# A hybrid HGRN2/retention step on one core: the first pass of each of the seven half-size products keeps its place in program order on TensorE

## The chip, the core and the metric

The kernel runs on one core of one Trainium2 chip. The metric is the device time in microseconds (us), median of the runs; for the kernel before it is 1810.23 us over three runs (1810.15 to 1811.55).

## What is computed

Two layers of a backbone over 640 tokens (128 context tokens and 512 latent tokens, five tiles of 128), each with a token mixer and a SwiGLU feed-forward part. The mixer is cut here; the change lies in the feed-forward part of the second layer:

```python
def layer(x, cond, s0_h, s0_r, pos, p):
    ...
    y, S_a, S_b = token_mixers(h, p, s0_h, s0_r, pos)
    x = x + g_m * y
    h = rmsnorm(x, p["norm_ffn"]) * (1.0 + sc_f) + sh_f
    gate, up = jnp.split(h @ p["w_up"], 2, axis=-1)
    x = x + g_f * ((jax.nn.silu(gate) * up) @ p["w_down"])
    return x, S_a, S_b
```

`w_up` has 1024 rows and 2 x 2816 columns, that is 22 blocks of 128 columns for `gate` and 22 for `up`; everything is float32.

## The kernel before, in words

Every float32 operand of a large product is held as a pair of a rounded part and a rest (`wh` and `wl` for weights, the planes 0 and 1 of `hT`, or the pairs `eh`, for activations). A product of two such pairs is three matmuls: rounded by rounded, rounded by rest, rest by rounded. Weights come by DMA into `raw`, ScalarE (ACT) casts them into `wh` (L104), and VectorE (DVE) subtracts to get `wl` (L105). Four buffers of each are kept (`W_BUFS`).

In the second layer `PLAIN` leaves two of the 22 column blocks to ordinary products. The other 20 go through `seven` (L701): the block of `gate` and the block of `up` for 640 tokens are one 2 x 2 arrangement of half-size blocks (half of the 1024 rows, half of the 640 tokens), computed with seven half-size products instead of eight. The price is sums and differences: of the tokens once per layer, of the weights by VectorE (`sums`, L113, four per block), and of the products by VectorE on their way out. `CH[1]` cuts the 22 blocks into groups of 6, 6, 5 and 5; the two ordinary blocks stand in the first group, so the groups hold 4, 6, 5 and 5 calls of `seven`. After each group `cols_512` (L1187) multiplies the group's activations by rows of `w_down`, in matmuls over 512 columns (L1200 to L1202), and `x_add` adds them to `x`.

One call of `seven` works in two PSUM tiles, `sx` and `sy`, each of 1024 columns. Products go to the columns 0 to 319 or 512 to 831 of one of them. Here they are called, in the order in which the code issues them:

- x0: first half of `sx`; ScalarE then copies it (L721).
- x1: second half of `sx`; VectorE then subtracts (L723, v2).
- y0: first half of `sy`; VectorE then subtracts (L726, v3).
- y1: second half of `sy`; VectorE then subtracts (L728, c22).
- x0': added onto the first half of `sx`; ScalarE then takes its SiLU (L731).
- x1': second half of `sx`, afresh; VectorE then subtracts (L733), ScalarE takes the SiLU (L734).
- y1': added onto the second half of `sy`; VectorE then subtracts (L738), multiplies (L741), and the result is split into a pair by L742 (ScalarE) and L743 (VectorE).

Each product is one call of `prod` (L710): four slices of 128 rows, with three matmuls (here: passes) of 320 columns each, at L713, L714 and L715; twelve passes a product, 84 a call, 1680 in all. `sx` and `sy` come from a pool of four such tiles, so two calls are in flight.

The order of the instructions on each engine is not that of the code: a scheduler of the build chooses it from what depends on what. A dependence between a pass and a reader of `sx` or `sy` becomes a wait of TensorE. `pin` (L351) names one instruction to the scheduler that is to keep its place in program order; before the change it is used on some instructions of VectorE and ScalarE (the weight sums at L113 among them) and on none of TensorE.

Of the kernel before, what the change touches and what calls it, by code (L numbers as in the profile page):

```python
# [148 lines left out]
class Net:  # L149
# [551 lines left out]
    def seven(self, act):  # L701
        nc, W, E = self.nc, self.W, self.E
        mm, V = nc.tensor.matmul, nc.vector
        X, Y, T = self.ps("sx"), self.ps("sy"), self.ON("sv")
        x0, x1, y0, y1 = X[:, :HALF], X[:, 512:512 + HALF], Y[:, :HALF], Y[:, 512:512 + HALF]
        v2, v3, c12, c22 = (T[:, i * HALF:(i + 1) * HALF] for i in range(4))
        sg = self.B("sgf")
        s1, s2 = sg[:, :HALF], sg[:, HALF:TOK]

        def prod(o, w, j, h, first=True):  # L710
            hi, lo = (x[:, HK * j:HK * j + HK] for x in w)
            for k in range(HK):
                mm(o, hi[:, k], h[0][:, k], start=first and k == 0, stop=False, skip_group_check=True)  # L713
                mm(o, hi[:, k], h[1][:, k], start=False, stop=False, skip_group_check=True)  # L714
                mm(o, lo[:, k], h[0][:, k], start=False, stop=k == HK - 1, skip_group_check=True)  # L715
            if j:
                W.done()
            return 5.1e-3 * HALF
        a = W.get(W.used)
        yield prod(x0, a, 0, self.quarter(0, 0))  # L720
        nc.scalar.copy(v2, x0)  # L721
        yield prod(x1, a, 1, E[2])
        V.tensor_tensor(v2, x1, v2, op=ALU.subtract)  # L723
        b = W.get(W.used)
        yield prod(y0, b, 0, E[3])
        V.tensor_tensor(v3, v2, y0, op=ALU.subtract)  # L726
        yield prod(y1, b, 1, E[1])
        V.tensor_tensor(c22, v3, y1, op=ALU.subtract)  # L728
        c = W.get(W.used)
        yield prod(x0, c, 0, self.quarter(0, 1), False)  # L730
        nc.scalar.activation(s1, x0, AF.Silu)  # L731
        yield prod(x1, c, 1, self.quarter(1, 1))
        V.tensor_tensor(s2, x1, v3, op=ALU.subtract)  # L733
        nc.scalar.activation(s2, s2, AF.Silu)  # L734
        d = W.get(W.used)
        cost = prod(y1, d, 0, E[4], False)
        W.done()
        V.tensor_tensor(c12, v2, y1, op=ALU.subtract)  # L738
        at = self.B("act", F32R).rearrange("p (d t) -> p d t", d=2)
        fv = sg[:, TOK:]  # L740
        V.tensor_tensor(fv, sg[:, :TOK], T[:, TOK:], op=ALU.mult)  # L741
        nc.scalar.copy(at[:, 0], fv)  # L742
        V.tensor_tensor(at[:, 1], fv, at[:, 0].bitcast(F32), op=ALU.subtract)  # L743
        act.append(at)
        yield cost
# [703 lines left out]
```

## Time and profile before

| what | value |
|---|---|
| median of 3 runs | 1810.23 us (1810.15 to 1811.55) |
| profiled execution, its own time | 1810.44 us |
| its span in the profile | 1808.7 us |
| TensorE (PE) busy | 1765.9 us, 98% of the span |
| VectorE (DVE) busy | 1192.8 us, 66% |
| ScalarE (ACT) busy | 763.7 us, 42% |
| mean granted clock of TensorE | 0.997 of full speed |

The profile gives busy time by engine, the chain of work that ended last, groups of instructions with what ended the idle time before them, and a timeline. The time of the execution is its span and 1.7 us around it. A matmul's row shows 0.31 us for a pass of 320 columns, but passes overlap; what one costs is the distance from its start to the start of the next.

### The profile page before, as it was taken

Reading aid. Unit: us, or ns where it says so; the run is one execution under the profiler, and the core shown is the slowest. Engines: PE = TensorE matmul, PEld = TensorE weight load, DVE = VectorE, ACT = ScalarE, POOL = GpSimd, SP = SyncE. Lnnn points to the kernel's source line nnn. Section 1 sums busy time; section 2 is a strip of 40 time slices with the busy share of each in tenths; the row PEclk is TensorE's granted clock in tenths of the full one; section 3 lists DMA queues with packets and bytes.
Section 4 is the critical chain, followed back from the end, with each engine's and each line's share of the span. In section 5 each row is a group of like instructions: output and inputs, shape, how many; then the busy total and the mean of one; then the engine's idle time right before and its main releaser. Section 6 shows DMA issues by size and latency. Waiting matters only on the chain.

```text
span 1808.7 us, 29243 instructions
## 1 busy us (share of the span) xinstructions
PE 1765.9 (98%) x12019; PEld 1678.3 (93%) x12019; DVE 1192.8 (66%) x1874; ACT 763.7 (42%) x1299; POOL 49.8 (3%) x59
## 2 busy tenths in 40 slices
PE   7999999999999999999999999999999999999997
PEld 5999899998999989999899999999999989899896
DVE  6787958864854666565676656475377667666766
ACT  7685445543422212222256555455354324233242
POOL 1100000000000000000000000000000000000000
PEclk9999999999999999999999999999999999999999
DMA  9414233221533444444442121211211312223131
GB/s 335 153 51 156 76 105 111 86 70 56 163 112 117 152 155 141 144 147 134 134 129 73 51 71 54 67 53 56 70 36 47 112 47 88 82 71 100 53 105 59
DMA packets 201622, 181.96 MB, mean 101 GB/s; under 512 B 7072, under 2 KB 171136, under 8 KB 201488
## 3 DMA queue, kind: packets, MB, share of 16 engines
q1 hardware_dynamic: 196592, 177.57, 31.3%
q10 hardware_dynamic: 4640, 2.43, 0.5%
q8 instruction: 94, 1.54, 0.3%
q0 software_dynamic: 256, 0.09, 0.1%
q14 instruction: 40, 0.33, 0.1%
HBM read 175.35 MB, written 4.72 MB: 100 GB/s over the span
## 4 chain that ended last, share of the span: by engine, by line
PE 75%; DVE 11%; ACT 5%; issue 4%; DMA 3%; POOL 1%; SPq 0%; DVEq 0%; POOLq 0%; ACTq 0%
PE gw L780 24%; PE ga L1200 6%; PE ga L1201 6%; PE ga L1202 6%; PE ga L826 4%; PE ga L825 4%; PE ga L824 4%; PE pl L917 3%; PE sx L713 2%; DVE wl L105 2%; PE sx L715 2%; PE sx L714 2%; ACT wh L104 2%; PE sy L713 1%; PE sy L714 1%
## 5 line engine op out<-in xcount | busy, mean ns | idle before, releaser
L104 ACT CAST wh<-raw 128x1024 fp32r<-128x1024 f32 (+1 forms) x265 | 265.2, 1001 | 644.9 <-PE gw L780 177.1
L105 DVE TENSOR_TENSOR wl<-raw,wh 128x1024 fp32r<-128x1024 f32 (+1 forms) x265 | 306.2, 1163 | 260.4 <-ACT wh L104 257.7
L780 PE MATMUL gw<-hT,wh 128*128 128x320 f32 x2432 | 461.8, 311 | 0.0
L780 PEld LDWEIGHTS gw<-hT,wh 128*128 128x128 f32 x2432 | 380.3, 188 | 0.6
L780 PE MATMUL gw<-hT,wl 128*128 128x320 f32 x1216 | 277.3, 309 | 0.0
L780 PEld LDWEIGHTS gw<-hT,wl 128*128 128x128 f32 x1216 | 203.1, 188 | 0.0
L824 PE MATMUL ga<-wh,hT 128*128 128x256 f32 x640 | 185.5, 290 | 0.0
L825 PE MATMUL ga<-wl,hT 128*128 128x256 f32 x640 | 181.3, 283 | 0.0
L826 PE MATMUL ga<-wh,hT 128*128 128x256 f32 x640 | 181.2, 283 | 0.0
L552 DVE CUSTOM_DVE_ANT_0 junk<-adt,srow 128x1024 f32<-128x1024 f32 x128 | 156.2, 1221 | 3.2 <-DMA adt<-in_ada_t 1.3
L1200 PE MATMUL ga<-wh,act 128*128 128x512 f32 x360 | 141.8, 394 | 0.0
L1201 PE MATMUL ga<-wl,act 128*128 128x512 f32 x360 | 140.5, 390 | 0.0
L1202 PE MATMUL ga<-wh,act 128*128 128x512 f32 x360 | 138.8, 390 | 0.0
L824 PEld LDWEIGHTS ga<-wh,hT 128*128 128x128 f32 x640 | 122.4, 191 | 0.1
L825 PEld LDWEIGHTS ga<-wl,hT 128*128 128x128 f32 x640 | 122.4, 191 | 0.1
L826 PEld LDWEIGHTS ga<-wh,hT 128*128 128x128 f32 x640 | 122.3, 191 | 0.0
L1200 PEld LDWEIGHTS ga<-wh,act 128*128 128x128 f32 x360 | 67.5, 188 | 17.4 <-DVE xa L1143 4.0
L713 PE MATMUL sx<-hT,wh 128*128 128x320 f32 x240 | 77.0, 322 | 4.0 <-DVE sv L723 4.0
L1202 PEld LDWEIGHTS ga<-wh,act 128*128 128x128 f32 x360 | 67.6, 188 | 14.1
L1201 PEld LDWEIGHTS ga<-wl,act 128*128 128x128 f32 x360 | 67.6, 188 | 13.4 <-DVE wl L105 0.6
L917 PE MATMUL pl<-X 128*128 128x128 f32 x560 | 72.9, 277 | 5.2 <-ACT X L904 5.1
L1143 DVE TENSOR_TENSOR xa<-ga,gate 128x512 f32<-128x512 f32 (+1 forms) x100 | 56.2, 580 | 32.9 <-PE ga L1202 17.0
(278 smaller groups left out, 3480.8 us busy)
## 6 DMA issues: line engine op xcount, KB each, us to landing
raw<-in_w_in SPq DMA_DIRECT2D x72, 512.0 KB, 3.8
adt<-in_ada_t SPq DMA_DIRECT2D x64, 512.0 KB, 3.8
raw<-in_w_up SPq DMA_DIRECT2D x48, 512.0 KB, 3.8
raw<-in_w_up SPq DMA_DIRECT2D x80, 256.0 KB, 3.0
raw<-in_w_down SPq DMA_DIRECT2D x39, 512.0 KB, 3.7
adw<-in_ada_w SPq DMA_DIRECT2D x16, 512.0 KB, 10.5
adw<-in_ada_w SPq DMA_DIRECT2D x32, 256.0 KB, 3.0
raw<-in_w_out SPq DMA_DIRECT2D x16, 512.0 KB, 3.7
```

What stands on the lines that cost most here:

```text
L104: nc.scalar.copy(hi[:, :n], raw[:, :n])
L105: nc.vector.tensor_tensor(lo[:, :n], raw[:, :n], hi[:, :n].bitcast(F32), op=ALU.subtract)
L552: r = V.tensor_tensor_reduce(out=self.junk, in0=w[:, :DM], in1=self.srow[c], scale=1.0, scalar=0.0, op0=ALU.mult, op1=ALU.add, accum_out=( ...
L713: mm(o, hi[:, k], h[0][:, k], start=first and k == 0, stop=False, skip_group_check=True)
L780: mm(o, w[:, k], self.hT[:, d, k, sl], start=k == 0 and i == 0, stop=k == KT - 1 and i == 2)
L824: mm(o, a_hi, hi[:, j], start=i == 0, stop=False)
L825: mm(o, a_hi, lo[:, j], start=False, stop=False)
L826: mm(o, a_lo, hi[:, j], start=False, stop=i == nk - 1)
L917: nc.tensor.matmul(pl[:, i * P:(i + 1) * P], X[:, TOK + i * P:TOK + (i + 1) * P], X[:, i * P:(i + 1) * P], start=True, stop=True)
L1200: mm(o, a_hi, hi[:, j], start=i == 0, stop=False)
L1201: mm(o, a_hi, lo[:, j], start=False, stop=False)
L1202: mm(o, a_lo, hi[:, j], start=False, stop=i == nk - 1)
```

## The change

The first pass of each product, the one at slice 0 of rounded by rounded, is given to `pin`. No instruction is added or removed.

```diff
@@ -710,7 +710,9 @@
         def prod(o, w, j, h, first=True):
             hi, lo = (x[:, HK * j:HK * j + HK] for x in w)
             for k in range(HK):
-                mm(o, hi[:, k], h[0][:, k], start=first and k == 0, stop=False, skip_group_check=True)
+                r = mm(o, hi[:, k], h[0][:, k], start=first and k == 0, stop=False, skip_group_check=True)
+                if k == 0:
+                    self.pin(r)
                 mm(o, hi[:, k], h[1][:, k], start=False, stop=False, skip_group_check=True)
                 mm(o, lo[:, k], h[0][:, k], start=False, stop=k == HK - 1, skip_group_check=True)
             if j:
```

L714 and L715 of the kernel before are L716 and L717 of the changed one, and all later lines are two higher.

How the order moves on TensorE is shown at three places of one call of `seven`, the fourth of the second group. Its tiles are `sx_14259` and `sy_14260`; `wh_14162` and `wl_14163` are the weights of x0 and x1, `14196`/`14197` those of y0 and y1, `14229`/`14230` those of x0' and x1', `14249`/`14250` those of y1'. What stands in brackets is the engine whose count the instruction waits for.

TensorE before, from the end of x0 to the beginning of x1:

```order
L715 MATMUL sx_14259<-hT_12371,wl_14163 128x320
L713 MATMUL sy_14260<-hT_12371,wh_14196 128x320
L714 MATMUL sy_14260<-hT_12371,wh_14196 128x320
L715 MATMUL sy_14260<-hT_12371,wl_14197 128x320 [waits DVE_49]
L713 MATMUL sy_14260<-hT_12371,wh_14196 128x320
L713 MATMUL sx_14259<-eh_12948,wh_14162 128x320 [waits Activation_49]
L714 MATMUL sx_14259<-eh_12949,wh_14162 128x320
```

TensorE in the changed kernel, the same place:

```order
L716 MATMUL sx_14259<-hT_12371,wh_14162 128x320
L717 MATMUL sx_14259<-hT_12371,wl_14163 128x320
L713 MATMUL sx_14259<-eh_12948,wh_14162 128x320 [waits Activation_49]
L716 MATMUL sx_14259<-eh_12949,wh_14162 128x320
L717 MATMUL sx_14259<-eh_12948,wl_14163 128x320
```

Four passes of y0 stood between the last pass of x0 and the first of x1, which waits for ScalarE; now none does.

TensorE before, from the end of y0 into x0':

```order
L714 MATMUL sy_14260<-hT_12371,wh_14196 128x320
L715 MATMUL sy_14260<-hT_12371,wl_14197 128x320
L713 MATMUL sx_14259<-hT_12371,wh_14229 128x320 [waits DVE_49]
L714 MATMUL sx_14259<-hT_12371,wh_14229 128x320
L715 MATMUL sx_14259<-hT_12371,wl_14230 128x320
```

Here y1 came only after eight passes of x0'. TensorE in the changed kernel, from the end of y0:

```order
L716 MATMUL sy_14260<-hT_12371,wh_14196 128x320
L717 MATMUL sy_14260<-hT_12371,wl_14197 128x320
L713 MATMUL sy_14260<-eh_12964,wh_14196 128x320 [waits DVE_49]
L716 MATMUL sy_14260<-eh_12965,wh_14196 128x320
L717 MATMUL sy_14260<-eh_12964,wl_14197 128x320
```

Now y1 follows y0 at once, with a wait for VectorE, and x0' comes after y1 with no wait.

TensorE before, from the end of x0' to the beginning of x1':

```order
L715 MATMUL sx_14259<-hT_12371,wl_14230 128x320
L713 MATMUL sx_14388<-hT_12371,wh_14290 128x320 [waits Activation_49]
L714 MATMUL sx_14388<-hT_12371,wh_14290 128x320
L715 MATMUL sx_14388<-hT_12371,wl_14291 128x320 [waits DVE_49]
L713 MATMUL sy_14260<-eh_12993,wh_14249 128x320 [waits DVE_49]
L714 MATMUL sy_14260<-eh_12994,wh_14249 128x320
L715 MATMUL sy_14260<-eh_12993,wl_14250 128x320
L713 MATMUL sx_14259<-hT_12371,wh_14229 128x320 [waits Activation_49]
```

TensorE in the changed kernel, the same place:

```order
L716 MATMUL sx_14259<-hT_12371,wh_14229 128x320
L717 MATMUL sx_14259<-hT_12371,wl_14230 128x320
L713 MATMUL sx_14259<-hT_12371,wh_14229 128x320 [waits Activation_49]
L716 MATMUL sx_14259<-hT_12371,wh_14229 128x320
L717 MATMUL sx_14259<-hT_12371,wl_14230 128x320
```

Three passes of the next call's x0 and three of y1' stood between x0' and x1'; now x1' follows x0' at once. In the changed program each of the 140 products stands as twelve passes in a row, in the order x0, x1, y0, y1, x0', x1', y1', but for the first call of the groups two to four, whose x0 is parted once by six passes of `cols_512`. In the last call of each group passes of `cols_512` still stand between products: five ahead of y1 in the first two groups and three in the last two, and three ahead of x1' in all four. On VectorE, in most calls, L738 now stands ahead of the subtraction of the 512-wide weights (L105) instead of behind it, and one L105 and one L113 changed places; on ScalarE one cast of the 20 at L742 moved by one place; the DMA queue of SyncE and GpSimd keep their order.

## Rows read from the trace of the kernel before

**Rows 1.** The page: engines' busy times; the weight subtraction L105 (busy, mean ns, idle before).

```profile
PE 1765.9 (98%) x12019; PEld 1678.3 (93%) x12019; DVE 1192.8 (66%) x1874; ACT 763.7 (42%) x1299; POOL 49.8 (3%) x59
...
L105 DVE TENSOR_TENSOR wl<-raw,wh 128x1024 fp32r<-128x1024 f32 (+1 forms) x265 | 306.2, 1163 | 260.4 <-ACT wh L104 257.7
```

**Rows 2.** One period: stretch, length, busy by engine (count), clock, DMA share, GB/s.

```profile
1508.26:1521.64 13.38, 12.95 (x84) 12.32 (x85) 10.37 (x16) 5.54 (x8) 0.00 (x0) 1.00 0.27 80
```

**Rows 3.** Tile sx, 1380 to 1770 us: what TensorE's idle time ended with (us, times).

```profile
  DVE sv L723: 11.1, 23
  ACT sv L721: 3.9, 20
  ACT sgf L731: 2.8, 16
```

**Rows 4.** Timeline, TensorE: end of x0, then first, second and twelfth x1 passes.

```profile
1517.19 0.31 PE L715 MATMUL sx<-hT,wl 128*128 128x320 f32 x1
...
1518.02 0.42 PE L713 MATMUL sx<-eh,wh 128*128 128x320 f32 x1
1518.27 0.31 PE L714 MATMUL sx<-eh,wh 128*128 128x320 f32 x1
...
1519.73 0.31 PE L715 MATMUL sx<-eh,wl 128*128 128x320 f32 x1
```

**Rows 5.** Timeline, ScalarE: the copy of x0 and the SiLU of x0'.

```profile
1517.54 0.43 ACT L721 COPY sv<-sx 128x320 f32<-128x320 f32 x1 [0.80 <-PE sx L715]
...
1525.73 0.43 ACT L731 ACTIVATE sgf<-sx 128x320 f32<-128x320 f32 x1
```

**Rows 6.** Timeline, TensorE and VectorE: end of y0, L723, two x0' passes.

```profile
1520.90 0.31 PE L715 MATMUL sy<-hT,wl 128*128 128x320 f32 x1
...
1521.10 0.48 DVE L723 TENSOR_TENSOR sv<-sx,sv 128x320 f32<-128x320 f32 x1
...
1521.64 0.41 PE L713 MATMUL sx<-hT,wh 128*128 128x320 f32 x1 [0.43 <-DVE sv L723]
1521.89 0.30 PE L714 MATMUL sx<-hT,wh 128*128 128x320 f32 x1
```

**Rows 7.** Timeline, TensorE: end of x0', first and second passes of x1'.

```profile
1525.11 0.31 PE L715 MATMUL sx<-hT,wl 128*128 128x320 f32 x1
...
1526.21 0.41 PE L713 MATMUL sx<-hT,wh 128*128 128x320 f32 x1
1526.46 0.31 PE L714 MATMUL sx<-hT,wh 128*128 128x320 f32 x1
```

**Rows 8.** Timeline: end of x1' (TensorE), its reader L733, and L726 (VectorE).

```profile
1527.92 0.31 PE L715 MATMUL sx<-hT,wl 128*128 128x320 f32 x1
...
1528.34 0.49 DVE L733 TENSOR_TENSOR sgf<-sx,sv 128x320 f32<-128x320 f32 x1 [1.26 <-PE sx L715]
...
1522.10 0.48 DVE L726 TENSOR_TENSOR sv<-sv,sy 128x320 f32<-128x320 f32 x1
```

**Rows 9.** Timeline, ScalarE: L721 of each group's first and last call.

```profile
1384.76 0.43 ACT L721 COPY sv<-sx 128x320 f32<-128x320 f32 x1
1423.96 0.43 ACT L721 COPY sv<-sx 128x320 f32<-128x320 f32 x1 [0.80 <-PE sx L715]
1478.03 0.43 ACT L721 COPY sv<-sx 128x320 f32<-128x320 f32 x1
1544.28 0.43 ACT L721 COPY sv<-sx 128x320 f32<-128x320 f32 x1 [0.80 <-PE sx L715]
1598.36 0.43 ACT L721 COPY sv<-sx 128x320 f32<-128x320 f32 x1 [0.36 <-PE sx L715]
1651.03 0.43 ACT L721 COPY sv<-sx 128x320 f32<-128x320 f32 x1 [0.80 <-PE sx L715]
1698.46 0.43 ACT L721 COPY sv<-sx 128x320 f32<-128x320 f32 x1 [0.36 <-PE sx L715]
1751.14 0.43 ACT L721 COPY sv<-sx 128x320 f32<-128x320 f32 x1 [0.80 <-PE sx L715]
```

## The prediction, written before the changed kernel ran

> **What bounds the kernel now.** I read the page first. TensorE is busy for 98% of the span [rows 1]. Work on other engines therefore matters only where TensorE stands still for it, and a change that adds or removes no instruction can only change those stands. The next view is one period of the stage that the change touches, from the first x0' pass of one call of `seven` to that of the next. It lasts 13.38 us for 84 passes, with VectorE busy for 10.37 us, ScalarE for 5.54 us, and the granted clock at 1.00, its 2.4 GHz level [rows 2]. So TensorE bounds this stage too, with 3 us of room on VectorE. Third, the idle time of TensorE around the tile `sx` names what it waits for: VectorE's L723 for 11.1 us, ScalarE's L721 for 3.9 us in all 20 calls, and L731 for 2.8 us in 16 [rows 3]. These sums understate a stand, since the pass after a wait is late as well. Therefore I price stands from the distances of the starts in the timeline.
>
> **A pass and its plain cost.** From the second to the twelfth pass of x1 ten starts take 1.46 us, 0.146 us each [rows 4].
>
> **The stands of a call before.** I take one call, the fourth of the second group.
> - x1 waits for L721, ScalarE's copy of x0. From the last x0 pass to the first x1 pass there are 0.83 us [rows 4]. Four y0 passes lie between, so five steps of 0.146 (0.73) are work and 0.10 is a stand. The next pass comes 0.25 us later instead of 0.146, another 0.10 [rows 4]. Together 0.20 us.
> - x0' waits for L723, the reader of x1. Between the last y0 pass and the first x0' pass there are 0.74 us, a stand of 0.59 us, and 0.25 us to the second pass, 0.10 more [rows 6]. Together 0.70 us. L723 was late: it began 1.37 us after the last x1 pass [rows 4, 6].
> - x1' waits for L731, the reader of x0'. With six passes between there are 1.10 us, seven steps are 1.02, so 0.08 and again 0.10 for the second pass [rows 7]. Together 0.18 us.
> - y1 and y1' cost nothing: eight passes of x0' and longer pieces cover their readers.
>
> Sum 1.08 us. The period without stands is 13.38 - 1.08 = 12.30 us, which is 84 passes of 0.146.
>
> **What the change removes.** The stand of x0' goes entirely: x0' now follows y1, and y1's wait for L726 already implies that L723 is done, since both are VectorE's and L723 comes first. That is 0.70 us less per call. The piecemeal stands at x1 and x1' (0.20 and 0.18) go in their present form.
>
> **What the change adds.** The waits are the same as before; what moves is what stands ahead of the waiting pass. TensorE works in order, so everything behind that pass waits with it, the other tile's products and the next call's included.
> - x1 directly behind x0. The path is: ScalarE begins L721 0.35 us after the last x0 pass has begun, needs 0.43 us, and x1 begins 0.05 us later, 0.83 us in all [rows 4, 5]. None of the four passes lies in it any more, so the stand is 0.83 - 0.146 = 0.68, plus 0.10 for the second pass: 0.79 us.
> - x1' directly behind x0'. L731 takes 0.43 us, and x1' begins 0.05 us after its end [rows 5, 7]. Its reader is on ScalarE as well and would begin 0.35 us after the last pass, as L721 did: again 0.79 us. The cast that kept ScalarE busy ahead of L731 waits for weights that y1 frees; with all twelve x0' passes now behind y1, it is over before x0' is.
> - y1 directly behind y0. The trace never shows VectorE free at this place, so I price it by the nearest rows. VectorE's L733 begins 0.42 us after the last pass of its product; L726 takes 0.48 us [rows 8]; the waiting pass begins 0.06 us after VectorE's end, as x0' did after L723 [rows 6]. That is 0.96 us, a stand of 0.81, and with 0.10 for the second pass 0.92 us. The lower bound is ScalarE's response of 0.35 in place of 0.42. The upper bound lets L723 be as late as now, 1.37 us after x1's last pass: then L726, which came 1.00 us behind L723 with one weight sum between them [rows 6, 8], begins at 2.37, where y0 (twelve passes, 1.75 us, and 0.42) would allow 2.17. So up to 0.2 us more. I take 0.92, because the stands themselves give VectorE more time ahead of L723.
> - y1' behind x1': its reader L728 has all of x0' and x1' (24 passes, 3.5 us) and the stand at x1' to finish. Nothing. The swaps of L105 and L113 with L728 and L738 on VectorE fall in the same cover; if it were gone, the price would be one L105, 1.16 us on average [rows 1], a call.
> - x0 of the next call and y0 use tiles and weights freed a call or more ago. Nothing.
>
> New stands: 0.79 + 0.92 + 0.79 = 2.50 us. The new period is 12.30 + 2.50 = **14.80 us**, 1.42 over the steady one of before.
>
> **The sum.** Not all calls were steady. From the first to the last L721 of the four groups there are 39.20, 66.25, 52.67 and 52.68 us, 210.80 us for 16 periods, 13.18 on average [rows 9]. Now 16 x 14.80 = 236.8 us: **+26.0**. The first x1 of each group lies outside these periods: 4 x (0.79 - 0.20) = **+2.4**. In the last call of each group wide passes still stand ahead of y1 and x1'. Passes of 512 columns, by columns, would take 0.146 x 512/320 = 0.23 us (an estimate from the row), so three cover 0.7 and five 1.2 us; what is left is 0 to 0.2 us each, about what these places cost before: **0**. Uncovered they would be 4 x 1.7 = 6.8 us, the upper bound.
>
> Together +28.4 us. The profiled execution took 1810.44 us, so 1838.8; the median of the runs lies 0.2 us below it, so **1838.6 us**. No later stage can give this back: the wide products that follow run on TensorE too.
>
> **Rivals.**
> - *The waits don't bind (faster).* Place: the first pass of x1, x1' and y1. The two products of a tile lie in different halves of it, so the reader of one half need not hold up writes to the other. If the waits were met by the time TensorE arrives, only the gain would be left: the decisive point is a reader's path below 0.146 us instead of 0.83. Then a period is 12.30: 16 x 12.30 = 196.8, 14.0 below 210.8, and 4 x 0.20 less at the first calls: 1810.23 - 14.8 = 1795.4 us. For it speaks that the halves are disjoint. Against it: with four passes in between, x1 stood in all 20 calls [rows 3], and began just behind the reader's end [rows 4, 5]. Chance 0.04. The Trainium skill, PSUM — Partial Sum Buffer, section "PSUM bank collisions raise a hardware error", asks for a guard "by bank × quadrant", and by its bank of 512 fp32 values the two halves lie in different banks. By that rule alone these waits would not be needed, and the time would be this rival's; the row shows that the program waits all the same, by tile.
> - *VectorE falls behind (much slower).* If the new order lets one more weight subtraction (1.16 us, [rows 1]) stand ahead of L726 or L728 when TensorE needs it, each call pays 0.2 to 1.16 us more: 1842.6 to 1861.8 us. For it speaks L723's lateness now; against it VectorE's 10.37 us in a period that grows to 14.80. Chance 0.10, of which I leave 0.06 beyond my range.
> - *Nothing changes.* If the moved stands only replaced each other, or the order on the chip's queue made no difference, the time would be 1810 us. The rows of the order speak against it: the passes that covered the waits are gone at all 20 calls. Chance 0.03.
>
> **How the numbers follow.** The forecast has 0.83, the rivals 0.04, 0.10 and 0.03. If the late second pass came only half as often as assumed, 20 x 3 x 0.05 = 3 us fall away; if never, 6 us; with the faster response at y1 20 x 0.07 = 1.4 us: low end 1831. Upward, 0.2 us at y1 in 20 calls are 4 us, and most of the uncovered last calls 5 us: high end 1848. Outside lie the faster rival, no change and the worse part of the second, 0.13 together, and some error of pricing. A measurement of this kernel can tell about 0.2%, 3.6 us, from no change. Faster 0.04, the same 0.03, slower 0.93.
>
> **What would show it.** In the changed profile the period of `seven` should be near 14.8 us; the idle ahead of L713 should name L721, L731 and now L726 some 20 times each, with about 0.5 us or more a time, and L723 no longer; the number of passes and the pitch of 0.146 should stay; the granted clock should stay at 1.00. A step is wrong if x1 begins less than 0.8 us behind x0's last pass, if L726 begins more than 0.5 us behind y0's last pass, or if y1' waits. The prediction is wrong if the period stays at or under 13.4 us.

## The result, and the profile after

The changed kernel takes 1836.81 us (median of 4 runs, 1836.49 to 1837.19) against 1810.19 us of the kernel before (4 runs): a ratio of 1.0146, 95% interval 1.0128 to 1.0163, or 26.6 us more. The forecast was 1838.6 us. The profiled execution spans 1835.1 us, 26.4 more than before.

The head of the page of the changed kernel, with span, busy times, share of the span and number of instructions:

```profile
span 1835.1 us, 29217 instructions
...
PE 1767.4 (96%) x12019; PEld 1675.6 (91%) x12019; DVE 1192.2 (65%) x1874; ACT 767.0 (42%) x1299; POOL 49.7 (3%) x59
```

Against [rows 1] no engine has an instruction more, and none is busy for over 4 us longer. TensorE is busy for 1.5 us longer in a span that is 26.4 us longer: it stands.

The view by tile says for what. First `sx`, then `sy`, from 1380 to 1800 us: what ended the idle time of the engine ahead of an instruction on the tile (us, times):

```profile
  PE sx L717: 84.5, 64
  ACT sv L723: 25.9, 40
  ACT sgf L733: 22.1, 36
```

```profile
  DVE sv L728: 24.1, 34
  PE sy L717: 20.1, 22
```

In [rows 3] the first name was VectorE's L723, which is L725 now; it is gone from the list. ScalarE's L721 (now L723) and L731 (now L733) have grown, and L726 (now L728) is new. Each place counts twice here, for the weight load and for the pass: 40 is 20 calls. The view of waits, which lists TensorE's queue for weight loads apart (engine, tile and line, waited for: us, times, longest), gives the stands almost as they are:

```profile
PEld sx L713 <- ACT sv L723: 15.6, 20, 0.8
PEld sy L713 <- DVE sv L728: 14.5, 18, 1.2
PEld sx L713 <- ACT sgf L733: 13.7, 20, 0.8
```

That is 43.8 us: 0.78 each at x1, 0.8 at y1, and 0.8 at x1' in 16 calls with 0.2 in the four last ones. The timeline shows the three places of one call (start, length, engine, line, operation, tiles, idle time ahead):

```profile
1526.76 0.31 PE L717 MATMUL sx<-hT,wl 128*128 128x320 f32 x1
...
1527.11 0.43 ACT L723 COPY sv<-sx 128x320 f32<-128x320 f32 x1 [1.24 <-PE sx L717]
...
1527.59 0.41 PE L713 MATMUL sx<-eh,wh 128*128 128x320 f32 x1 [0.52 <-ACT sv L723]
1527.84 0.31 PE L716 MATMUL sx<-eh,wh 128*128 128x320 f32 x1
...
1529.30 0.31 PE L717 MATMUL sx<-eh,wl 128*128 128x320 f32 x1
...
1529.67 0.48 DVE L725 TENSOR_TENSOR sv<-sx,sv 128x320 f32<-128x320 f32 x1
...
1531.06 0.31 PE L717 MATMUL sy<-hT,wl 128*128 128x320 f32 x1
1531.41 0.49 DVE L728 TENSOR_TENSOR sv<-sv,sy 128x320 f32<-128x320 f32 x1 [0.66 <-PE sy L717]
...
1531.95 0.41 PE L713 MATMUL sy<-eh,wh 128*128 128x320 f32 x1 [0.58 <-DVE sv L728]
1532.20 0.30 PE L716 MATMUL sy<-eh,wh 128*128 128x320 f32 x1
...
1533.66 0.31 PE L717 MATMUL sy<-eh,wl 128*128 128x320 f32 x1
...
1533.81 0.31 PE L713 MATMUL sx<-hT,wh 128*128 128x320 f32 x1
...
1535.42 0.31 PE L717 MATMUL sx<-hT,wl 128*128 128x320 f32 x1
1535.77 0.44 ACT L733 ACTIVATE sgf<-sx 128x320 f32<-128x320 f32 x1 [0.81 <-PE sx L717]
...
1536.26 0.42 PE L713 MATMUL sx<-hT,wh 128*128 128x320 f32 x1 [0.53 <-ACT sgf L733]
1536.51 0.32 PE L716 MATMUL sx<-hT,wh 128*128 128x320 f32 x1
```

x1 comes 0.83 us behind the last pass of x0, y1 0.89 behind that of y0, x1' 0.84 behind that of x0', and the pass after each comes 0.25 later instead of 0.15. x0', which stood for 0.70 us in [rows 6], follows y1 after 0.15 us. The period from one first x1 pass to the next (columns as in [rows 2]):

```profile
1527.59:1542.32 14.73, 13.11 (x84) 12.32 (x84) 10.33 (x15) 5.73 (x9) 0.00 (x0) 1.00 0.34 99
```

It was 13.38 us there. The granted clock is 1.00 in both, so the clock has no part in it.

For the comparison of all kernels I add up the stands of the 20 calls as in the prediction: the distance of a product's first pass from the pass ahead, less 0.147 us, plus what the second pass is late. Each cell is the sum in us, worked out from the starts of all passes on `sx` and `sy` in the profiled execution. "Stage" is the time from the first of these passes to the last.

| kernel | x1 | y1 | x0' | x1' | y1' | all | stage | median |
|---|---|---|---|---|---|---|---|---|
| before | 4.0 | 0.3 | 7.7 | 3.0 | 0.5 | 16.3 | 379.8 | 1810.19 |
| changed | 15.7 | 14.5 | 0.0 | 13.5 | 0.0 | 43.9 | 408.2 | 1836.81 |
| only y0 in place | 15.6 | 1.1 | 0.0 | 3.6 | 0.4 | 20.9 | 383.8 | 1814.45 |
| only x0' in place | 3.9 | 20.2 | 0.0 | 4.2 | 0.0 | 28.7 | 395.0 | 1826.43 |
| x0 and y1' in place | 3.9 | 2.1 | 0.0 | 14.5 | 0.0 | 20.7 | 384.1 | 1814.87 |
| changed, x0 copied twice | 24.8 | 14.5 | 0.0 | 13.5 | 0.0 | 53.0 | 417.3 | 1847.42 |
| changed, late casts | 15.7 | 14.4 | 0.0 | 19.7 | 0.0 | 50.0 | 414.4 | 1844.37 |
| two tiles, late casts | 0.0 | 0.0 | 0.0 | 0.2 | 1.6 | 2.0 | 365.3 | 1795.87 |
| two tiles | 0.0 | 0.4 | 0.5 | 3.7 | 0.8 | 5.8 | 369.7 | 1799.56 |
| two tiles, x1' ahead of y1' | 0.0 | 0.0 | 0.0 | 0.9 | 25.2 | 26.3 | 389.8 | 1819.56 |

("All" has the small sums at x0 and y0 as well.) Stands explain 27.6 of the 28.3 us by which the stage grew. The span grew by 1.9 less: the stage begins 1.2 us earlier after the change, a difference that arose in the first 400 us of the program, where nothing was changed (1.9 us by 46 us, of which 0.7 were lost again by 396), and what follows the stage is 0.7 shorter. The experiments ran in three groups, and in each the kernel before ran beside them, with medians of 1809.1 to 1809.7 us; the ratios below go by those.

### The profile page after: what moved, and what is told of

Its sections match the earlier page's. It is cut to its first block, busy times and chain, and to the rows that moved or that the text cites. A ratio compares the mean times of both kernels' runs of the same rounds, so it can differ in the third digit from the quotient of the medians.

```text
span 1835.1 us, 29217 instructions
## 1 busy us (share of the span) xinstructions
PE 1767.4 (96%) x12019; PEld 1675.6 (91%) x12019; DVE 1192.2 (65%) x1874; ACT 767.0 (42%) x1299; POOL 49.7 (3%) x59
## 4 chain that ended last, share of the span: by engine, by line
PE 80%; DVE 9%; ACT 5%; issue 2%; DMA 1%; POOL 1%; SPq 0%; POOLq 0%; DVEq 0%; ACTq 0%
PE gw L782 24%; PE ga L1202 6%; PE ga L1203 5%; PE ga L1204 5%; PE ga L828 4%; PE ga L827 4%; PE ga L826 4%; PE sx L713 3%; PE pl L919 3%; PE sx L716 3%; PE sx L717 3%; PE sy L713 2%; PE sy L717 2%; PE sy L716 2%; DVE wl L105 1%
## 5 line engine op out<-in xcount | busy, mean ns | idle before, releaser
L105 DVE TENSOR_TENSOR wl<-raw,wh 128x1024 fp32r<-128x1024 f32 (+1 forms) x265 | 307.3, 1162 | 257.9 <-ACT wh L104 257.4
```

The costliest lines, as they stand in the source:

```text
L105: nc.vector.tensor_tensor(lo[:, :n], raw[:, :n], hi[:, :n].bitcast(F32), op=ALU.subtract)
```

## The experiments

My theory after the result: the stand at a product is **the path of the reader ahead of it less the passes of the other tile that stand between**. The change took these passes away at x1, y1 and x1'. The rivals were that one of the waits alone makes the loss, that TensorE gives the time back elsewhere, and that the price lies in the fixed order itself and not in the readers. The diffs of experiments 1 to 4 and 7 start from the changed kernel (2 and 3 with the argument `pin` of 1), that of 5 from the kernel before, those of 6 and 8 from 5.

**1. Only y0's first pass keeps its place.** Of the seven products one is tied; the others may move as before.

```diff
-        def prod(o, w, j, h, first=True):
+        def prod(o, w, j, h, first=True, pin=False):
...
-                if k == 0:
+                if pin and k == 0:
                     self.pin(r)
...
-        yield prod(y0, b, 0, E[3])
+        yield prod(y0, b, 0, E[3], pin=True)
```

> Only the first pass of y0 keeps its place; x1 then follows x0 at once, the rest of the order is as before the change. Theory (a stand is the reader's path less the passes between): x1 stands 0.79 instead of 0.20 us, but the four passes that covered it now come behind x1 and cover L723, so that in the steady calls x0' stands 0 to 0.1 instead of 0.70 us. Where x0' hardly stood before (about 8 of the 20 calls) 0.59 us are lost each. Together 3 to 6 us over before, about 1815 us. Rival (each place has its own price, whatever else moves): 20 x 0.59 = 12 us over before, 1822 us.

Measured: 1814.45 us, ratio 1.0027 (1.0017 to 1.0037). In the table x1 stands as in the changed kernel, 0.78 us in all 20 calls, and x0' no longer. +11.6 at x1 against -7.7 at x0': the passes of y0 stand behind x1 instead of ahead of it, so the cover has moved and is not lost. The order alone makes the stand at x1, and it gives x0' its time back.

**2. Only x0' keeps its place.**

```diff
-        yield prod(x0, c, 0, self.quarter(0, 1), False)
+        yield prod(x0, c, 0, self.quarter(0, 1), False, pin=True)
```

> Only the first pass of x0' keeps its place; y1 then follows y0 at once and x0' follows y1; x0 and x1' keep most of their cover. Theory: y1 waits for L726, which stands behind L723 and one weight sum on VectorE. With only eight y0 passes behind x1 and L723 as late as before (1.37 us behind the last x1 pass), L726 ends at about 2.85 us and y1 stands some 1.7 us, against 0.70 us of x0' before; where L723 is not late, about 0.9 us. Together 14 to 22 us over before, about 1828 us. Rival (each place has its own price): 20 x (0.92 - 0.55) = 7 us over before, 1817 us.

Measured: 1826.43 us, 1.0093 (1.008 to 1.0107). y1 has lost its cover, and here it stands longer than in the changed kernel, 1.40 us in steady calls (the expectation had 1.7). The timeline of TensorE and VectorE shows why:

```profile
1499.89 0.68 DVE L113 TENSOR_TENSOR raw<-raw 128x512 f32<-128x512 f32 x1
...
1500.50 0.48 DVE L725 TENSOR_TENSOR sv<-sx,sv 128x320 f32<-128x320 f32 x1
1500.59 0.31 PE L717 MATMUL sy<-hT,wl 128*128 128x320 f32 x1
1500.90 0.68 DVE L113 TENSOR_TENSOR raw<-raw 128x512 f32<-128x512 f32 x1
1501.50 0.48 DVE L728 TENSOR_TENSOR sv<-sv,sy 128x320 f32<-128x320 f32 x1
...
1502.03 0.41 PE L713 MATMUL sy<-eh,wh 128*128 128x320 f32 x1 [1.13 <-DVE sv L728]
```

x1 does not stand for long here, so VectorE comes late to L725, behind a weight sum, and then to L728, which begins 0.91 us after y0's last pass; in the changed kernel it began 0.35 after it. This is the prediction's rival of a late VectorE, 0.55 us a call, inside the 0.2 to 1.16 us that it gave; weight sums hold VectorE here, and not the weight subtraction that the rival named. The stands account for 12.4 us of the 15.1 by which the stage is longer than before; two waits for weights inside products, 1.7 us in the view by tile, are part of the rest.

**3. x0 and y1' keep their place.** Now x1' has nothing between, but x1 and y1 keep their cover.

```diff
-        yield prod(x0, a, 0, self.quarter(0, 0))
+        yield prod(x0, a, 0, self.quarter(0, 0), pin=True)
...
-        cost = prod(y1, d, 0, E[4], False)
+        cost = prod(y1, d, 0, E[4], False, pin=True)
```

> Only the first passes of x0 and y1' keep their place; x1' then follows x0' at once, x1 keeps its four y0 passes. Theory: x1' stands 0.79 instead of 0.18 us, 0.61 us a call; six passes come later, which gives VectorE up to 0.4 us more ahead of L723, so x0' stands 0.25 to 0.7 us as against 0.70. Together 4 to 12 us over before, about 1818 us. Rival (the order on one tile costs nothing, VectorE sets the period): within 2 us of before.

Measured: 1814.87 us, 1.0027 (1.0016 to 1.0038). x1' stands as in the changed kernel, 0.80 us. x0' should have kept 0.25 to 0.7 us by the expectation and has nothing: in this order L725 begins 0.37 us behind the last x1 pass in the steady calls, as in the changed kernel; in the kernel before L723 began 1.37 us behind it. So each place can be made to stand by itself; yet what is lost or gained at x0' depends on where VectorE is, and the three prices don't simply add up.

**4. The changed kernel, with ScalarE's copy of x0 made twice.** The same copy is written twice, which lengthens the reader and nothing else.

```diff
         nc.scalar.copy(v2, x0)
+        nc.scalar.copy(v2, x0)
```

> The changed kernel with ScalarE's copy of x0 made twice into the same place. Theory: the reader's path ahead of x1 grows by one copy, 0.40 to 0.43 us, in all 20 calls: 8 to 8.6 us over the changed kernel, about 1845 us. Rival (VectorE's queue sets the period, ScalarE has room): within 2 us of the changed kernel, about 1837 us.

Measured: 1847.42 us against the kernel before, ratio 1.0211 (1.0197 to 1.0225); that is 10.6 us over the changed kernel, and the stage is 9.1 longer, as is the profiled execution (1845.96 us; the five runs lie between 1845.75 and 1849.45). One call in the timeline of TensorE and ScalarE (L724 is the second copy):

```profile
1529.86 0.31 PE L717 MATMUL sx<-hT,wl 128*128 128x320 f32 x1
...
1530.21 0.43 ACT L723 COPY sv<-sx 128x320 f32<-128x320 f32 x1 [1.28 <-PE sx L717]
1530.67 0.43 ACT L724 COPY sv<-sx 128x320 f32<-128x320 f32 x1
...
1531.15 0.41 PE L713 MATMUL sx<-eh,wh 128*128 128x320 f32 x1 [0.97 <-ACT sv L724]
```

The second copy begins 0.46 us behind the first, and x1 comes 0.46 later: 1.29 instead of 0.83 us behind x0. 20 x 0.46 = 9.2 us. The reader's path is paid in full, microsecond for microsecond; nothing hides any of it.

**5. No place kept, and neighbours on different tiles.** If the wait costs only because neighbours share a tile, it should vanish when they don't. x0 takes the first half of `sx`, x1 the first of `sy`, y0 the second of `sx`, y1 the second of `sy`; then x0', y1' and last x1', which lies in y0's place; `v3` is subtracted from it as before. Nothing keeps its place by force. Because VectorE and ScalarE are to read in time, the buffers of the weights are also given back, and the casts of the next ones issued, only behind the readers of a pair.

```diff
-        x0, x1, y0, y1 = X[:, :HALF], X[:, 512:512 + HALF], Y[:, :HALF], Y[:, 512:512 + HALF]
+        x0, x1, y0, y1 = X[:, :HALF], Y[:, :HALF], X[:, 512:512 + HALF], Y[:, 512:512 + HALF]
...
-            if j:
-                W.done()
...
         V.tensor_tensor(v2, x1, v2, op=ALU.subtract)
+        W.done()
...
         V.tensor_tensor(c22, v3, y1, op=ALU.subtract)
+        W.done()
...
-        yield prod(x1, c, 1, self.quarter(1, 1))
-        V.tensor_tensor(s2, x1, v3, op=ALU.subtract)
-        nc.scalar.activation(s2, s2, AF.Silu)
-        d = W.get(W.used)
-        cost = prod(y1, d, 0, E[4], False)
-        W.done()
+        d = W.get(W.used + 1)
+        yield prod(y1, d, 0, E[4], False)
         V.tensor_tensor(c12, v2, y1, op=ALU.subtract)
+        cost = prod(y0, c, 1, self.quarter(1, 1))
+        V.tensor_tensor(s2, y0, v3, op=ALU.subtract)
+        W.done(2)
+        nc.scalar.activation(s2, s2, AF.Silu)
```

> The kernel before, without the new pins, with the products dealt out over the two tiles in turn: x0 in the first half of sx, x1 in the first half of sy, y0 in the second half of sx, y1 in the second half of sy, x0' onto x0, y1' onto y1, then x1' in the second half of sx; and the weights' sums and casts of the next call are issued behind the readers L723 and L728 instead of ahead of them. Each product is again twelve passes in a row. Theory (a stand is the reader's path less the passes between): twelve passes of the other tile, 1.76 us, lie ahead of every wait, more than the 0.83 or 0.96 us of a reader's path, so the stands of the calls go: 12.3 us a call, 1795 us (1793 to 1801). Rival (contiguous products or VectorE's queue cost the time): 1810 us or more.

Measured: 1795.87 us, 0.9923 (0.9909 to 0.9936): faster than both kernels, by 13.8 us against its own runs of before and by 40.9 against the changed one. Two lines show it: of the page, and of the view of stretches (columns as in [rows 2]) one period, from one first x1 pass to the next.

```profile
PE 1754.7 (98%) x12019; PEld 1677.0 (93%) x12019; DVE 1191.3 (66%) x1874; ACT 767.9 (43%) x1299; POOL 49.7 (3%) x59
```

```profile
1500.06:1512.38 12.32, 12.32 (x87) 12.32 (x86) 10.48 (x17) 5.73 (x9) 0.00 (x0) 1.00 0.30 85
```

The period is 12.32 us, and TensorE is busy for all of it. The waits by tile are as many as before: five of a call's seven products still wait for a reader. In nearly all calls they are met when TensorE arrives, since twelve passes of the other tile stand ahead of each; what is left is 1.6 us at y1'.

**6. The same tiles and order of the code, with the weights given back where they were.** The order on TensorE is again the scheduler's, since nothing keeps its place.

```diff
+            if j:
+                W.done()
...
-        W.done()
...
-        W.done()
...
+        W.done()
         V.tensor_tensor(s2, y0, v3, op=ALU.subtract)
-        W.done(2)
```

> The same tiles and order of products, with the weights' sums and casts issued where they were. On VectorE three weight sums and two weight subtractions then stand between L726 and L728, and y1' waits for L728. Theory: L728 ends about 5.4 us behind the last y0 pass, where 24 passes cover 3.6 us: y1' stands up to 1.9 us a call, 20 to 38 us in all, and the time is 1815 to 1833 us. Rival (only the tile that a product stands in counts): 1795 us.

Measured: 1799.56 us, 0.9945 (0.9933 to 0.9958). The expectation was far off. Its mechanism is there: VectorE comes late to a reader, as this stretch of its timeline shows.

```profile
1517.05 0.48 DVE L726 TENSOR_TENSOR sv<-sv,sx 128x320 f32<-128x320 f32 x1
1517.45 1.89 DVE L113 TENSOR_TENSOR raw<-raw 128x512 f32<-128x512 f32 x3
...
1519.38 2.36 DVE L105 TENSOR_TENSOR wl<-raw,wh 128x1024 fp32r<-128x1024 f32 x2
...
1521.66 0.48 DVE L728 TENSOR_TENSOR sv<-sv,sy 128x320 f32<-128x320 f32 x1
```

(L726 reads y0 and L728 y1 here.) What I had overlooked is that in such calls the program has x1' ahead of y1', so twelve more passes stand ahead of the product that waits for L728. I had taken the order of one call for that of all 20. The late casts of experiment 5, with the order on TensorE that comes with them (there each product stands as twelve passes, here many are parted), are worth 3.7 us, and the two tiles the rest.

**7. The changed kernel, with the late casts alone.** The other half of experiment 5, on the old tiles.

```diff
-            if j:
-                W.done()
...
         V.tensor_tensor(v2, x1, v2, op=ALU.subtract)
+        W.done()
...
         V.tensor_tensor(c22, v3, y1, op=ALU.subtract)
+        W.done()
...
         V.tensor_tensor(s2, x1, v3, op=ALU.subtract)
+        W.done()
```

> The changed kernel, pins and products on their old tiles, with the weights' sums and casts of the next call issued behind L723, L728 and L733 instead of ahead of them: the half of the two-tiles edit that concerns VectorE alone. Theory (the three stands are the readers' paths, which were answered at once already): 1834 to 1838 us, within 3 us of the changed kernel. Rival (the gain with two tiles came from VectorE's queue): about 1796 to 1815 us.

Measured: 1844.37 us, 1.019 (1.0173 to 1.0207). The rival, that late casts make the gain, falls; but the theory missed by 7 us too. x1' stands 1.18 instead of 0.80 us in 16 calls:

```profile
1553.57 1.05 ACT L104 CAST wh<-raw 128x1024 fp32r<-128x1024 f32 x1 [2.53 <-DVE raw L113]
...
1553.78 0.31 PE L717 MATMUL sx<-hT,wl 128*128 128x320 f32 x1
1554.52 0.43 ACT L733 ACTIVATE sgf<-sx 128x320 f32<-128x320 f32 x1
...
1555.00 0.42 PE L713 MATMUL sx<-hT,wh 128*128 128x320 f32 x1 [0.91 <-ACT sgf L733]
```

The late cast now lies just ahead of ScalarE's SiLU, which begins 0.74 us after x0' instead of 0.35. What is queued ahead of a reader belongs to its path.

**8. Two tiles and late casts, each product in its place, x1' directly ahead of y1'.** x1' lies in the first half of `sy`, so that y1' follows it on its own tile: one pair of neighbours, and three pairs on different tiles.

```diff
-                mm(o, hi[:, k], h[0][:, k], start=first and k == 0, stop=False, skip_group_check=True)
+                r = mm(o, hi[:, k], h[0][:, k], start=first and k == 0, stop=False, skip_group_check=True)
+                if k == 0:
+                    self.pin(r)
...
-        d = W.get(W.used + 1)
-        yield prod(y1, d, 0, E[4], False)
-        V.tensor_tensor(c12, v2, y1, op=ALU.subtract)
-        cost = prod(y0, c, 1, self.quarter(1, 1))
-        V.tensor_tensor(s2, y0, v3, op=ALU.subtract)
-        W.done(2)
-        nc.scalar.activation(s2, s2, AF.Silu)
+        yield prod(x1, c, 1, self.quarter(1, 1))
+        V.tensor_tensor(s2, x1, v3, op=ALU.subtract)
+        W.done()
+        nc.scalar.activation(s2, s2, AF.Silu)
+        d = W.get(W.used)
+        cost = prod(y1, d, 0, E[4], False)
+        W.done()
+        V.tensor_tensor(c12, v2, y1, op=ALU.subtract)
```

> The two-tiles kernel with pins, late casts and one step changed: x1' goes before y1', in the first half of sy, so that y1', in the second half of sy, follows another product on its own tile once a call. Theory: y1' stands for the reader of x1' on VectorE, 0.85 to 0.92 us in each of 20 calls, and nothing else stands: 17 to 18 us over the two-tiles kernel's 1795.9, 1811 to 1814 us. Rival (the halves of a tile don't matter, only where casts are issued): 1796 us.

Measured: 1819.56 us, 1.0057 (1.0042 to 1.0072). Of seven products with their place kept only the one that follows a neighbour on its own tile stands to speak of (25.2 of 26.3 us), so keeping the place costs nothing by itself. The expected size was again too small: y1' stands 1.49 us in 16 calls instead of about 0.9:

```profile
1542.44 1.23 DVE L105 TENSOR_TENSOR wl<-raw,wh 128x1024 fp32r<-128x1024 f32 x1 [0.59 <-ACT wh L104]
...
1542.59 0.31 PE L717 MATMUL sy<-hT,wl 128*128 128x320 f32 x1
...
1543.58 0.48 DVE L735 TENSOR_TENSOR sgf<-sy,sv 128x320 f32<-128x320 f32 x1
...
1544.12 0.42 PE L713 MATMUL sy<-eh,wh 128*128 128x320 f32 x1 [1.22 <-DVE sgf L735]
```

An L105 that had begun 0.15 us before the last pass of x1' holds VectorE, and L735 begins 0.99 us after that pass. In the last call of each group, where VectorE is idle, it begins 0.35 us after it.

## Why the prediction was right

The time, the sign and the mechanism came out as forecast; the steps one by one:

- **The period without stands, 12.30 us.** 14.73 less the three stands (0.78 + 0.85 + 0.80) is 12.30, and experiment 5, in which next to nothing stands, has periods of 12.32.
- **The stand of x0' goes.** Right: 7.7 us in all 20 calls before, 0.0 after. L725 is no wait of TensorE's any more; y1 waits for the subtraction behind it.
- **x1 and x1', 0.79 us each.** Measured 0.78 and 0.80. Experiment 4 shows that the price is the reader's own path.
- **y1, 0.92 us.** The one term that was mis-sized: measured 0.85 in steady calls, the lower bound that the prediction named. It took VectorE's response from L733 before, 0.42 us [rows 8], for lack of a free VectorE at this place; L728 begins 0.35 us after the last pass. The same reader as in [rows 8], now L735, still begins 0.41 after its own product (1537.98 to 1538.39), so the reader taken as the nearest row was another kind (see the last section). 16 x 0.07 are 1.1 us. The first call of all is an exception, with 1.20 us: there a weight subtraction, begun at 1387.04, holds VectorE until L728 begins at 1388.18, which is the second rival in one call.
- **VectorE gains time from the stands.** Right, and it kept the second rival away: L725 began 1.37 us after x1 before and begins 0.37 after it now (1529.30 to 1529.67). Where x1 hardly stands, in experiment 2, VectorE does come late, and it costs 0.55 us a call.
- **The sum.** From the first to the last L723 of the four groups there are 44.56, 73.67, 58.93 and 58.94 us. The ends of the second group, in the timeline of ScalarE:

```profile
1482.91 0.43 ACT L723 COPY sv<-sx 128x320 f32<-128x320 f32 x1 [0.36 <-PE sx L717]
...
1556.58 0.43 ACT L723 COPY sv<-sx 128x320 f32<-128x320 f32 x1 [1.24 <-PE sx L717]
```

  Together 236.1 us where the forecast had 236.8 and [rows 9] give 210.8: +25.3 instead of +26.0. The first calls of the groups give 4 x 0.58 = 2.3 (forecast 2.4). In the last calls y1 stands 0.08 to 0.24 us and x1' 0.18, about 1.4 us in all, where x0' and x1' stood 1.1 us before: +0.3, forecast 0.
- **From the stage to the whole.** The stage grew by 28.3 us where the sum said 28.4. That it is so close is in part luck: the parts measured above add up to 27.9, with y1 priced 1.1 too high, the first call and the last calls 0.6 too low, and 0.4 us of the stage lie in none of them. The 1.8 us by which the forecast is too high lie outside the stage, where 1.9 us less make the profiled span only 26.4 longer. 1.2 of these arose ahead of the stage, where nothing was changed; that they fell on this side is chance, since the start of the stage differs by up to 3.3 us among the profiled kernels here.
- **The rivals.** That the waits don't bind is refuted by 20 stands of 0.78 us at x1, each ending 0.05 us behind the reader's end. The Trainium skill, PSUM — Partial Sum Buffer, section "PSUM bank collisions raise a hardware error", has PSUM guarded by bank × quadrant, which would guard the two halves apart. The trace does not speak against that as a rule of the chip; it shows that this program waits for the whole tile. Experiment 5 comes to the time of that rival, 1795.87 against 1795.4 us, by putting other passes ahead of the waits, with the guards kept. Whether the halves could be guarded apart on the old tiles was not tried. That nothing changes is refuted by the time.

## What to carry to other kernels

A wait of TensorE costs the path of the reader (how soon it begins, what is queued ahead of it on its engine, its own length) less the work that stands between; here about 0.8 us for each bare wait. Before an order is fixed, look for consecutive products on one tile: the freedom to move others between them may be what hides the reader, and where the order is to be fixed, neighbours want different tiles. Price a moved wait for every place at once, since a stand at one gives the engines behind it time at the next (experiments 1 and 2), and read the order of every call, not of one (experiment 6).

## What was not expected of the hardware

Two readers on the same engine answer at different speeds: VectorE's L728 begins 0.35 us after the start of the last pass it waits for, and L735 0.41, although both come to an idle VectorE. The traces show what goes with it. L735 waits for two other engines, TensorE and ScalarE: the wait for TensorE then stands on an instruction of its own ahead of the subtraction, which itself carries the wait for ScalarE. Where the subtraction carries the wait for TensorE itself, as L728 does, it begins sooner. Experiment 7 has both for one line, L723, with ScalarE waited for in the first of these calls and not in the second:

```profile
1617.64 0.31 PE L717 MATMUL sx<-eh,wl 128*128 128x320 f32 x1
...
1618.05 0.49 DVE L723 TENSOR_TENSOR sv<-sx,sv 128x320 f32<-128x320 f32 x1 [0.31 <-PE sx L717]
...
1632.78 0.31 PE L717 MATMUL sx<-eh,wl 128*128 128x320 f32 x1
...
1633.13 0.49 DVE L723 TENSOR_TENSOR sv<-sx,sv 128x320 f32<-128x320 f32 x1 [0.49 <-PE sx L717]
```

Over all ten traces, subtractions on an idle VectorE that had to wait for TensorE began 0.34 to 0.35 us after the pass in all 165 cases in which they carry that wait themselves, and 0.41 to 0.42 us in 152 of the 154 in which it stands on an instruction ahead. No run changed this alone.

A wait of TensorE also cost a little more than itself: the waiting pass lasted 0.41 us instead of 0.31, and the next one came 0.25 us behind it instead of 0.15, at each of the three places and in experiments 2, 4, 7 and 8 alike.
